# Embedding gate: three of four output-tile pairs by seven half products in place of eight, their operand sums formed in the last down projection, the fourth pair by column halves at both ends

## The chip, the cores and the metric

The kernel runs on one core of a Trainium2 chip. The metric is device microseconds of one execution; the time before is the median of three runs, 1333.55 us (1332.72 to 1333.56). All matmuls run on TensorE (PE in the profile); VectorE is DVE, ScalarE is ACT, GpSimd is POOL, and SP is the engine that issues most DMAs. The kernel is written in a tile framework that tracks tiles, places the semaphores and sets the order of each engine's instructions with a scheduler of its own; the order is fixed when the program is built, and each engine works through its list in that order.

## The reference, cut to what matters

One step of a one-layer decoder for 64 sampled tokens and 512 prompt tokens, 576 rows in all, with a model width of 1024. After the token mixers the layer does this:

```python
hf = rmsnorm(h, w['norm_ffn'])
h = h + (jax.nn.silu(hf @ w['w_gate']) * (hf @ w['w_up'])) @ w['w_down']
gate = jax.nn.sigmoid(rmsnorm(h, w['norm_ple']) @ w['w_ple_gate'])
h = h + gate * (p.astype(h.dtype) @ w['w_ple_proj'])
...
y_prompt = rmsnorm(hp, norm_final)
```

The change is in the line of `gate`, a product of 576 x 1024 by 1024 x 1024 in float32. The product `p @ w_ple_proj` is made much earlier in the kernel and waits in DRAM as eight tiles `pp_d`.

## The kernel before

Everything is held transposed: 128 partitions are 128 features, and the 576 tokens lie along the free axis. A tensor of 1024 features is eight tiles of 128 x 576. The residual is `hs[0..7]`.

**Float32 by three passes.** A float32 operand is split into a high part `hi` (rounded to float32r by an ACT copy) and a low part `lo` (the source less `hi`, by DVE or POOL, or, where the engine is given as "D", by a negated ACT copy and an accumulating DMA that POOL issues). A product is the sum of hi·hi, hi·lo and lo·hi. `split` (L193) and `below` (L185) do this; all ACT copies have line L93, and the `lo` parts lines L191 and L213. For a tile of 128 outputs over 1024 inputs this is 8 input tiles times 3 passes.

**The gate and up projections** of the feed-forward part are made by `seven` (L1443): two output tiles at a time form a 2 x 2 block matrix (two halves of the inputs, `a11` to `a22` being 128 x 512 blocks of the weights), the tokens are cut in two halves `N1` and `N2` of 288, and the eight half products are made as seven, with sums of weight blocks (`s1`, `s2`, `s4`, and `a21` in place) and sums of the data (`T1` to `T4`, split once ahead). Each half product is `product` (L1428), 12 matmuls of 288 columns at line L1432. The seven are made in the order 1, 6, 4, 7, 5, 2, 3. Two PSUM tiles take them: `ab` (parts a, b) and `cd` (parts c, d), each 1024 columns. Step 7 adds into b, which step 6 wrote and DVE then read (`e[2]`, L1477); DVE reads b again as `e[3]` (L1483) after step 7; step 2 adds into a, in the same tile as b, and in the built program its first matmul waits for that read. In the same way the first matmul of step 5 (part c) waits for DVE's read of part d. `weave` (L1502) keeps two such blocks in flight; there are nine gate and nine up blocks, in two stretches, each followed by a down projection, `down` (L1520), of 8 tiles with 72 or 60 matmuls of 288 columns (L241). Its result is scaled on DVE (`dn`), added to `hs[c]` on POOL (L1526), and in the last `down` the function `after` (L1306) makes the split operand `xhi`, `xlo` of the next product and its squares `hsq`, which POOL sums up.

**The embedding gate** (L1541 to L1601) is made directly: for the token columns 0 to 320, and then for 320 to 576, all eight output tiles one after the other, each with 24 matmuls (L1577, L1578, L1579). Weights are loaded and split in the first pass and kept for the second. For each tile DVE scales by the reciprocal norm (L1583), ACT takes the sigmoid, and `embed` multiplies by the tile `pl` of the embedding product (L1556), adds to `hs[c]` (L1557), takes the square and sums it up on POOL (L1563). After each pass the final norm follows: `rstd_by_token` (L329) sums the squares over the partitions by matmuls with one column (L339), takes root and reciprocal, spreads the result over the partitions by transposes (L347), and eight tiles are scaled (six on DVE, L1600, two on POOL, L1598) and stored. For the first pass this lies beside the matmuls of the second.

## Time and profile before

| | us |
|---|---|
| median of three runs | 1333.55 |
| the profiled execution's own time | 1329.48 |
| its span, first to last instruction | 1327.7 |
| last matmul of the down projection begins its last group of four | 1259.17 |
| first matmul of the embedding gate | 1259.69 |
| last matmul of the embedding gate | 1316.30 |
| the weave of the second stretch, one pair of blocks (168 matmuls), from 1148.22 to 1171.20 | 22.98 |

The profiled execution took 1329.48 us, 4.07 less than the median of the runs; 1.78 of it lies outside the span. A timeline row gives the start, the length of the group, the engine, the line, the tiles (output, then inputs), the shape, the count, and in brackets idle time ahead of it with what ended that. Matmuls overlap their neighbours, so that the rate of a series is read from one start to the next and not from the length. The squares' sums (L339) show twice as many records as there are instructions.

### The profile page before, as it was taken

How to read it: one execution, taken by the hardware profiler on the slowest of the kernel's cores; microseconds unless marked ns; L12 is line 12 of the kernel's file. 1: busy time of each engine (PE TensorE's matmuls, PEld its weight loads, DVE VectorE, ACT ScalarE, POOL GpSimd, SP SyncE). 2: the span in 40 equal slices, each digit the busy share in tenths (PEclk: the TensorE clock that was granted, in tenths of full speed). 3: DMA queues.
4: the chain of work that ended last, by engine and by line, in shares of the span. 5: the costliest groups of instructions: out<-in, count | busy, mean ns of one | idle time of the engine just before them, and what ended most of it. 6: DMA issues, size and time to landing. Idle time of an engine off the chain costs nothing.

```text
span 1327.7 us, 26629 instructions
## 1 busy us (share of the span) xinstructions
PE 1224.9 (92%) x10429; PEld 1125.1 (85%) x10429; DVE 885.8 (67%) x1569; ACT 632.0 (48%) x1274; POOL 615.4 (46%) x584
## 2 busy tenths in 40 slices
PE   6897899999989978899989989999999999999997
PEld 5786797889968966788769878999999999999996
DVE  6649665878696876953456576858895138883464
ACT  6565436543654374343444364455553225553363
POOL 5426513642265136122445665647565345654642
PEclk9898999799978979979989989999999999999998
DMA  5322241334232322353454541253342224424322
GB/s 167 127 65 72 78 116 54 98 96 119 73 103 79 83 72 78 103 180 106 132 182 131 201 151 59 78 161 106 98 113 89 81 83 114 116 66 136 99 89 72
DMA packets 96764, 140.29 MB, mean 106 GB/s; under 512 B 34960, under 2 KB 39312, under 8 KB 96640
## 3 DMA queue, kind: packets, MB, share of 16 engines
q1 hardware_dynamic: 93760, 133.36, 32.6%
q0 software_dynamic: 2304, 4.72, 2.1%
q8 instruction: 82, 1.34, 0.4%
q10 hardware_dynamic: 576, 0.52, 0.1%
q14 instruction: 42, 0.34, 0.1%
HBM read 106.10 MB, written 27.75 MB: 101 GB/s over the span
## 4 chain that ended last, share of the span: by engine, by line
PE 58%; DVE 19%; ACT 6%; issue 6%; DMA 4%; POOL 3%; SPq 0%; DVEq 0%; ACTq 0%; POOLq 0%
PE lin L241 12%; PE lin L1432 11%; PE lin L228 6%; PE lin L230 6%; PE lin L229 6%; DVE h L402 2%; DVE wl L191 1%; DVE Tt L683 1%; DVE tmp L681 1%; DVE wlo L213 1%; PE lin L1577 1%; PE lin L1578 1%; PE lin L1579 1%; DVE suv L838 1%; DMA raw<-wts 1%
## 5 line engine op out<-in xcount | busy, mean ns | idle before, releaser
L213 POOL TENSOR_TENSOR wlo<-raw,whi 128x512 fp32r<-128x512 f32 (+1 forms) x92 | 125.8, 1368 | 303.6 <-ACT whi L93 235.0
L228 PE MATMUL lin<-xhi,whi 128*128 128x288 f32 (+1 forms) x784 | 242.1, 309 | 2.8 <-ACT whi L93 2.2
L230 PE MATMUL lin<-xhi,wlo 128*128 128x288 f32 (+1 forms) x784 | 240.2, 307 | 4.0 <-POOL wlo L213 2.3
L229 PE MATMUL lin<-xlo,whi 128*128 128x288 f32 (+1 forms) x784 | 239.6, 306 | 1.2 <-POOL xlo L191 1.1
L93 ACT ACTIVATE whi<-raw 128x512 fp32r<-128x512 f32 (+1 forms) x200 | 123.2, 616 | 211.0 <-PE lin L241 90.0
L228 PEld LDWEIGHTS lin<-xhi,whi 128*128 128x128 f32 (+1 forms) x784 | 149.5, 191 | 10.1 <-ACT whi L93 2.6
L230 PEld LDWEIGHTS lin<-xhi,wlo 128*128 128x128 f32 (+1 forms) x784 | 149.4, 191 | 7.9 <-POOL wlo L213 2.7
L229 PEld LDWEIGHTS lin<-xlo,whi 128*128 128x128 f32 (+1 forms) x784 | 149.4, 191 | 6.5 <-POOL xlo L191 2.4
L213 DVE TENSOR_TENSOR wlo<-raw,whi 128x512 fp32r<-128x512 f32 (+1 forms) x108 | 82.1, 761 | 74.2 <-PE lin L241 36.0
L1432 PE MATMUL lin<-T,wh 128*128 128x288 f32 x576 | 87.3, 296 | 2.0 <-DVE e L1477 1.3
L1432 PEld LDWEIGHTS lin<-T,wh 128*128 128x128 f32 x576 | 80.0, 189 | 3.2 <-DVE e L1477 1.6
L93 ACT ACTIVATE wh<-raw 128x512 fp32r<-128x512 f32 x72 | 45.1, 628 | 52.5 <-PE lin L1432 35.4
L191 POOL TENSOR_TENSOR wl<-raw,wh 128x512 fp32r<-128x512 f32 x36 | 57.3, 1592 | 11.7 <-ACT wh L93 6.2
L191 DVE TENSOR_TENSOR wl<-sw,wh 128x512 fp32r<-128x512 f32 x53 | 49.9, 941 | 9.3 <-ACT wh L93 5.2
L241 PE MATMUL lin<-ah,whi 128*128 128x288 f32 x352 | 54.7, 294 | 0.0
L241 PE MATMUL lin<-al,whi 128*128 128x288 f32 x352 | 54.4, 294 | 0.0
L241 PE MATMUL lin<-ah,wlo 128*128 128x288 f32 x352 | 54.2, 294 | 0.0
L681 DVE TENSOR_TENSOR tmp<-L,Tt 72x30 f32<-72x30 f32 (+14 forms) x120 | 49.9, 416 | 3.2
L1432 PE MATMUL lin<-T,wl 128*128 128x288 f32 x288 | 49.8, 297 | 0.6 <-DVE wl L191 0.6
L241 PEld LDWEIGHTS lin<-ah,whi 128*128 128x128 f32 x352 | 49.3, 188 | 0.0
L241 PEld LDWEIGHTS lin<-al,whi 128*128 128x128 f32 x352 | 49.2, 188 | 0.0
L241 PEld LDWEIGHTS lin<-ah,wlo 128*128 128x128 f32 x352 | 49.2, 188 | 0.0
(437 smaller groups left out, 3265.7 us busy)
## 6 DMA issues: line engine op xcount, KB each, us to landing
raw<-wts SPq DMA_DIRECT2D x271, 256.0 KB, 2.6
S<-s_wkv SPq DMA_DIRECT2D x8, 512.0 KB, 5.1
hd<-s_ssm SPq DMA_DIRECT2D x8, 512.0 KB, 4.6
o_ssm_s<-hd SPq DMA_DIRECT2D x8, 512.0 KB, 2.8
xbc_d<-E SPq DMA_DIRECT2D x12, 288.0 KB, 2.1
x<-xT SPq DMA_DIRECT2D x8, 288.0 KB
gate_d<-g SPq DMA_DIRECT2D x8, 288.0 KB, 2.5
bv_d<-rw SPq DMA_DIRECT2D x8, 288.0 KB
```

Source lines behind the costliest of these rows:

```text
L93: return S.activation(out, in_, func, bias=bias, scale=scale)
L191: eng.tensor_tensor(lo, src, hi.bitcast(F32), ALU.subtract)
L213: eng.tensor_tensor(lo[:, 0:n], raw[:, 0:n], hi[:, 0:n].bitcast(F32), ALU.subtract)
L228: T.matmul(ps[:, a:b], whi, xhi[:, a:b], start=first, stop=False)
L229: T.matmul(ps[:, a:b], whi, xlo[:, a:b], start=False, stop=False)
L230: T.matmul(ps[:, a:b], wlo, xhi[:, a:b], start=False, stop=last)
L241: T.matmul(ps[:, a:e], (hi, lo)[p][:, i * P:(i + 1) * P], xs[k + i][q][:, a:e], start=n == k + i == 0, stop=n == 2 and k + i == nk - 1, sk ...
L402: V.scalar_tensor_tensor(h[:], E[:, i:i + 600], w(i), h[:], ALU.mult, ALU.add)
L681: V.tensor_tensor(o, L[:, jx:jx + 1, jx + 1:32].to_broadcast([NB, jx, n]), Tt[:, 0:jx, jx:jx + 1].to_broadcast([NB, jx, n]), ALU.mult)
L683: V.tensor_tensor(Tt[:, 0:jx, jx + 1:32], Tt[:, 0:jx, jx + 1:32], o, ALU.subtract)
L838: V.scalar_tensor_tensor(dst, sv[h, jj, 0, e], PC[h, jj, 7 + g:8 + g], dw[h, jj], ALU.mult, ALU.add)
L1432: T.matmul(ps, (hi, lo)[p][:, k * P:(k + 1) * P], OPS[n][k][q], start=first and p == q == k == 0, stop=p == 1 and k == 3, skip_group_check ...
```

## The change

The gate's eight output tiles become four pairs. Pairs 0, 1 and 2 (tiles 0 to 5) are made by a new function `joined`, which does what `seven` does for the gate projection, one block after the other, with the same `product`. Tiles 6 and 7 are made by `plain` as before, with 24 matmuls each for `N1` ahead of the joined pairs and 24 each for `N2` at their end. All matmuls of the gate are now 288 columns wide: 3 x 84 joined and 4 x 24 plain, 348, against 192 of 320 and 192 of 256 columns before.

The sums of the data `T1` to `T4` are made by a new function `operands`, for each of the last four tiles of the last down projection. The embedding, the square and its sum are put off (`put_off`, `catch_up`, with a table `CU` of how many to take up after each step); for tiles 0 to 3 the adds to `hs[c]` go from DVE to POOL, and the squares are summed in two pairs only, so that six tiles of squares go into each final norm where three went before. The final norm of `N1` is written between the two plain tiles of `N2`. In the weave, the split weights get four buffers in place of three and the small tiles `e` six in place of eight, since the pool `cm` now lives on to the end; the embedding tiles `pl`, the plain weights and the squares take the places of the feed-forward tiles `ah`, `al`, and so are loaded only when the last down projection has read those. In the last down projection's last tile the add to `hs[7]` goes from POOL to DVE. The early load of the square root's table ahead of the last final norm is left out.

```diff
     def product(ps, w, n, first, eng):
-        hi, lo = split(w[:], cm, ("wh", "wl"), [P, 512], lo_eng=eng, bufs=3)
+        hi, lo = split(w[:], cm, ("wh", "wl"), [P, 512], lo_eng=eng, bufs=4)
...
+    CU = ((0,0,1,1,0,0,0),(0,1,1,0,0,0,0),(0,1,1,0,1,1,1))
+    PLE_ENG = ((V, V, G, V, "D", G, V), (V, V, G, V, "D", G, V), (V, V, G, V, "D", G, V))
...
+    def operands(k):
+        t0, t1, t2, t3, t4 = (cm.tile([P, HALF], F32, tag="e", name=nm("t"), bufs=6) for _ in range(5))
+        ha, hb = hs[k], hs[k + 4]
...
+        act(t0[:], ha[:, N2], AF.Identity, scale=ga)
+        V.scalar_tensor_tensor(t1[:], ha[:, N1], ga, t0[:], ALU.mult, ALU.subtract)
+        V.scalar_tensor_tensor(t2[:], hb[:, N2], gb, t1[:], ALU.mult, ALU.add)
+        V.scalar_tensor_tensor(t3[:], hb[:, N2], gb, t0[:], ALU.mult, ALU.subtract)
+        V.scalar_tensor_tensor(t4[:], hb[:, N1], gb, t2[:], ALU.mult, ALU.subtract)
...
-            G.tensor_tensor(hs[c][:], hs[c][:], t[:], ALU.add)
+            (V if last and c == 7 else G).tensor_tensor(hs[c][:], hs[c][:], t[:], ALU.add)
             if last:
-                after(c, hs[c], "norm_ple", pools[-1], "f", 9, st)
+                after(c, hs[c], "norm_ple", fp, "f", 6, st)
+                if c > 3:
+                    operands(c - 4)
...
+    def embed(c, t, sq, w, eng=V):
+        act(t[:, w], t[:, w], AF.Sigmoid)
+        V.tensor_tensor(t[:, w], t[:, w], PL[c][:, w], ALU.mult)
+        eng.tensor_tensor(hs[c][:, w], hs[c][:, w], t[:, w], ALU.add)
+        if c < 7:
+            act(sq[:, w], hs[c][:, w], AF.Square)
+        else:
+            V.tensor_tensor(sq[:, w], hs[c][:, w], hs[c][:, w], ALU.mult)
...
+            if c in (0,2):
+                G.tensor_tensor(SQ[c][:], SQ[c][:], SQ[c + 1][:], ALU.add)
+                summed.append(c + 1)
...
+        for n, step in enumerate("1647523"):
...
+            elif step == "7":
+                product(b, a21, "T3", False, on["7"])
+                e[3] = kt()
+                V.tensor_tensor(e[3][:], b, e[1][:], ALU.add)
+                joins(sb, 2 * p + 1, N1, d, e[3], SQ[2 * p + 1])
...
+    t6, t7 = spare("al8", "pg"), spare("ah9", "pg")
+    for i, t in enumerate((t6, t7)):
+        plain(i, N1, t)
+    for p in range(3):
+        joined(p)
+    plain(0, N2, t6)
+    catch_up(5)
+    store(N1, False)
+    plain(1, N2, t7)
+    catch_up(5)
+    store(N2, True)
```

The scheduler puts the instructions in a new order at three places that matter below. The first is on PE, in the weave of the second stretch. Here `lin_13224` is the tile `ab` of one block and `lin_13379` that of the next one; `T_1592` and `T_1593` are the high and the low part of `T3`, so that these rows are step 7, and `wh_13381`, `wl_13382` are the split weights of the next block's step 1. First the rows that leave their place:

```order
 L1432 MATMUL lin_13080<-xhi_9757,wl_13282 128x288
 L1432 MATMUL lin_13225<-T_1594_10206,wl_13301 128x288 x4
-L1432 MATMUL lin_13224<-T_1592_10204,wh_13326 128x288 x4
-L1432 MATMUL lin_13224<-T_1593_10205,wh_13326 128x288 x4
-L1432 MATMUL lin_13224<-T_1592_10204,wl_13327 128x288 x4
 L1432 MATMUL lin_13379<-xhi_9471,wh_13381 128x288
 L1432 MATMUL lin_13379<-xhi_9511,wh_13381 128x288
```

And, eight matmuls further on in the same piece of the list of PE, where they now stand:

```order
 L1432 MATMUL lin_13379<-xlo_9553,wh_13381 128x288
 L1432 MATMUL lin_13379<-xlo_9594,wh_13381 128x288
+L1432 MATMUL lin_13224<-T_1592_10204,wh_13326 128x288 x4
+L1432 MATMUL lin_13224<-T_1593_10205,wh_13326 128x288 x4
+L1432 MATMUL lin_13224<-T_1592_10204,wl_13327 128x288 x4
 L1432 MATMUL lin_13379<-xhi_9471,wl_13382 128x288
 L1432 MATMUL lin_13379<-xhi_9511,wl_13382 128x288
```

Step 7 stood ahead of all 12 matmuls of the next block's step 1 and now stands ahead of its last four; right behind those, in both programs, comes step 2 of the block `lin_13224`.

The second place is the end of the list of PE. Before, `lin_15244` is the last tile of the gate, `lin_15281` the final norm of the second pass:

```order
L1579 MATMUL lin_15244<-xhi_14472,wp_14933 128x256
L1577 MATMUL lin_15244<-xhi_14561,wp_14932 128x256
L1578 MATMUL lin_15244<-xlo_14562,wp_14932 128x256
L1579 MATMUL lin_15244<-xhi_14561,wp_14933 128x256
L339 MATMUL lin_15281<-ones,sq_15210 64x1 x4
L339 MATMUL lin_15281<-ones,sq_15243 64x1 x4
L339 MATMUL lin_15281<-ones,sq_15277 64x1 x4
L347 MATMUL lin_15281<-ident,rn_2487_15294 128x128 x2
```

Now `lin_15338` is tile 7 of `N2`, `lin_15275` the final norm of `N1` and `lin_15368` that of `N2`:

```order
L339 MATMUL lin_15275<-ones,sq_14681 64x1 x6
L339 MATMUL lin_15275<-ones,sq_14682 64x1 x6
L339 MATMUL lin_15275<-ones,sq_14683 64x1 x6
L339 MATMUL lin_15275<-ones,sq_14684 64x1 x6
L1604 MATMUL lin_15338<-xhi_14504,wp_14656 128x288
L1602 MATMUL lin_15338<-xhi_14611,wp_14655 128x288
L1603 MATMUL lin_15338<-xlo_14612,wp_14655 128x288
L1604 MATMUL lin_15338<-xhi_14611,wp_14656 128x288
L339 MATMUL lin_15368<-ones,sq_14679 64x1 x2
L339 MATMUL lin_15368<-ones,sq_14681 64x1 x6
L339 MATMUL lin_15368<-ones,sq_14682 64x1 x6
L347 MATMUL lin_15275<-ident,rn_2516_15312 128x128 x3
```

The sums of the first half's final norm now stand four matmuls ahead of the end of the gate, and its transposes behind it. Two more groups of them stand further ahead, 6 and 16 matmuls long, so that 46 matmuls of one column lie ahead of the gate's last product where 18 lay before.

The third place is the end of the list of DVE. Before, `pg_15269` is the gate of the last tile and `h_9161` the residual `hs[7]`:

```order
L1583 TENSOR_TENSOR pg_15269<-lin_15244,rstd_14622 128x256
L1556 TENSOR_TENSOR pg_15269<-pg_15269,pl_14583 128x256
L1557 TENSOR_TENSOR h_9161<-h_9161,pg_15269 128x256
L1561 TENSOR_TENSOR sq_15277<-h_9161 128x256
L344 RECIPROCAL rn_2487_15294<-rn_2487_15294 128x2
L1600 SCALAR_TENSOR_TENSOR h_8706<-h_8706,pv,lin_15281 128x256
```

Now `pg_14686` is the gate of tile 7, and `lin_15275` the spread norm of `N1`:

```order
L1607 TENSOR_TENSOR pg_14686<-lin_15338,rstd_14712 128x288
L1575 TENSOR_TENSOR pg_14686<-pg_14686,pl_14663 128x288
L1576 TENSOR_TENSOR h_9161<-h_9161,pg_14686 128x288
L1679 SCALAR_TENSOR_TENSOR h_8706<-h_8706,pv,lin_15275 128x288
L1679 SCALAR_TENSOR_TENSOR h_8771<-h_8771,pv,lin_15275 128x288
L1679 SCALAR_TENSOR_TENSOR h_8901<-h_8901,pv,lin_15275 128x288
L1679 SCALAR_TENSOR_TENSOR h_9031<-h_9031,pv,lin_15275 128x288
L1679 SCALAR_TENSOR_TENSOR h_9096<-h_9096,pv,lin_15275 128x288
L1679 SCALAR_TENSOR_TENSOR h_9161<-h_9161,pv,lin_15275 128x288
L1580 TENSOR_TENSOR sq_14684<-h_9161 128x288
L344 RECIPROCAL rn_2520_15405<-rn_2520_15405 128x3
```

The six scalings of the first half's final norm have come to stand between the last tile's add to the residual and the square of it.

More of the change, by code (lines that the diff above doesn't have):

```diff
@@ L1597, in hybrid_step, with store @@
+    def store(w, last):
+        ps = rstd_by_token(tuple(q for i, q in enumerate(SQ) if i not in summed), 1.0 / D, w.start, w.stop)
+        rl = ft("rs")
+        act(rl[:, w], ps)
+        for c in range(8):
+            h = hs[c][:, w]
+            if c in (2, 4):
                 act(h, h, AF.Copy, scale=par("norm_final", c))
-                G.tensor_tensor(h, h, rl, ALU.mult)
+                G.tensor_tensor(h, h, rl[:, w], ALU.mult)
             else:
                 V.scalar_tensor_tensor(h, h, par("norm_final", c), ps, ALU.mult, ALU.mult)
-            (nc.scalar if a and c % 2 else nc.sync).dma_start(A["yT"][c, :, a:b], h)
+            (nc.scalar if last and c % 2 else nc.sync).dma_start(A["yT"][c, :, w], h)
```

147 lines of the change are left out of this document (91 added, 56 removed).

## The prediction

> **What bounds the kernel now.** I read the page first, then the busy time by stretches around the change, then PE's timeline at their ends.
>
> ```profile
> span 1327.7 us, 26629 instructions
> ...
> PE 1224.9 (92%) x10429; PEld 1125.1 (85%) x10429; DVE 885.8 (67%) x1569; ACT 632.0 (48%) x1274; POOL 615.4 (46%) x584
> ```
>
> ```profile
> core 0: us, PE busy (x) PEld busy (x) DVE busy (x) ACT busy (x) POOL busy (x), PEclk, DMA share, GB/s
> 1148.22:1171.20 22.98, 22.74 (x169) 22.38 (x169) 20.62 (x32) 12.45 (x23) 14.03 (x11) 1.00 0.47 119
> 1259.69:1316.42 56.73, 56.08 (x470) 54.66 (x468) 33.08 (x63) 29.63 (x58) 21.39 (x20) 1.00 0.26 80
> 1316.42:1327.70 11.28, 1.85 (x28) 1.15 (x26) 4.30 (x11) 2.55 (x5) 1.48 (x3) 0.63 0.29 93
> ```
>
> PE is busy for 92% of the span. The second row is one pair of blocks of the weave, the third the whole gate, the fourth what follows its last product. In the weave and in the gate PE has the full clock (1.00) and is almost never idle; but in the weave DVE is busy for 20.62 of 22.98 us, in the present gate for only 33.08 of 56.73. So the gate is bound by the number of its products, and there is idle time on DVE and POOL that another form can use up. The last 11.28 us are a chain through DVE and ACT, with PE at 1.85.
>
> PE's timeline gives the rates:
>
> ```profile
> 1158.92 0.69 PE L1432 MATMUL lin<-xhi,wl 128*128 128x288 f32 x4
> 1159.57 0.77 PE L1432 MATMUL lin<-xhi,wh 128*128 128x288 f32 x4
> ...
> 1169.74 0.69 PE L1432 MATMUL lin<-xlo,wh 128*128 128x288 f32 x4
> 1170.27 0.69 PE L1432 MATMUL lin<-xhi,wl 128*128 128x288 f32 x4
> 1171.20 0.77 PE L1432 MATMUL lin<-xhi,wh 128*128 128x288 f32 x4 [0.24 <-DVE e L1483]
> ...
> 1277.80 0.31 PE L1578 MATMUL lin<-xlo,wp 128*128 128x320 f32 x1
> 1283.96 0.31 PE L1578 MATMUL lin<-xlo,wp 128*128 128x320 f32 x1
> ...
> 1292.10 0.52 PE L339 MATMUL lin<-ones,sq 128*64 128x1 f32 x12
> 1292.55 0.38 PE L1577 MATMUL lin<-xhi,wp 128*128 128x256 f32 x1
> ...
> 1301.07 0.28 PE L1577 MATMUL lin<-xhi,wp 128*128 128x256 f32 x1
> 1303.22 0.28 PE L1577 MATMUL lin<-xhi,wp 128*128 128x256 f32 x1
> ```
>
> From start to start, 42 products of 320 columns took 6.16 us, 0.1467 each; 18 of 256 took 2.15, 0.1194 each; four of 288 took 0.53 (1169.74 to 1170.27), 0.1325 each. Six column sums (twelve records) took 0.45, 0.075 each.
>
> **The change, part by part.** The sum is made against the profiled execution, 1329.48 us; the median of the runs lies 4.07 higher, and I carry the difference over unchanged. 0.2% is 2.7 us, about what a measurement of this kernel can tell from no change.
>
> Products: before 192 x 0.1467 + 192 x 0.1194 = 51.1; after 348 x 0.1325 = 46.1. That is -5.0, all of it on the path, since PE hardly idles there.
>
> Column sums: 46 stand ahead of the last product in place of 18, because only two pairs of squares are summed beforehand: 28 x 0.075 = +2.1. The three transposes of the first half leave the stretch: -0.3, estimated at a product's rate or less.
>
> Waits inside the stretch. Of the 56.73 us, 51.1 are products and 18 x 0.075 = 1.4 column sums; 4.2 are left, of which the 20 sums of the down projection's squares (1.5) and eight transposes (some 0.6) are work, so about 2.1 are waits and switches. What the joined pairs will wait has no row of its own; the nearest ones are those of the weave, which uses the same products in the same order:
>
> ```profile
> 1167.94 0.67 DVE L191 TENSOR_TENSOR wl<-sw,wh 128x512 fp32r<-128x512 f32 x1
> 1168.54 0.68 DVE L191 TENSOR_TENSOR wl<-raw,wh 128x512 fp32r<-128x512 f32 x1
> 1169.14 1.54 DVE L1498 TENSOR_TENSOR sa<-sa,rstd 128x288 f32<-128x288 f32 x1
> 1170.61 0.45 DVE L1483 TENSOR_TENSOR e<-lin,e 128x288 f32<-128x288 f32 x1
> ```
>
> ```profile
> 1168.69 1.67 POOL L1453 TENSOR_TENSOR sw<-raw,sw 128x512 f32<-128x512 f32 x1 [3.23 <-DVE wl L191]
> ```
>
> ```profile
> 939.97 1.93 PE L1432 MATMUL lin<-T,wh 128*128 128x288 f32 x8 [1.35 <-DVE e L1477]
> ```
>
> The rows 1170.27 and 1171.20 show the weave's wait at step 2: four products last 0.53, the next one starts 0.93 later, so 0.40 is lost until DVE has read `e[3]`; at the other block's step 2 it is 0.12 (1158.92 to 1159.57, 0.65), 0.52 in a pair of blocks. The weave has a second block to work on while it waits. A joined pair has none: step 7 waits for the read of `e[2]`, 2 for that of `e[3]`, 5 and 3 for those of d and c, and only the following pair's first eight products stand in between at one place. The lower bound for 252 such products is the weave's rate, 0.52 x 252 / 168 = 0.8. The upper one comes from the weave's start, where one wait alone was 1.35 (row 939.97): at two such waits in each pair, 8. I take 4.3, between the two and nearer the first: DVE is in order, and behind each put-off embedding it stands at the sigmoid's result from ACT, with `e[3]` queued behind it; ACT has a tile's square ahead of the copies that split the next pair's `a11`. Against the 2.1 of before this is +2.2, with ends -1.3 and +5.9.
>
> The front seam I cost at nothing. The sums for `T2` to `T4` of the last down tile come behind `hs[7]`, whose add moves from POOL to DVE:
>
> ```profile
> 1259.88 0.76 DVE L1525 TENSOR_TENSOR dn<-lin,rstd 128x576 f32<-128x576 f32 x1 [0.61 <-PE lin L241]
> ```
>
> ```profile
> 1260.72 1.44 POOL L1526 TENSOR_TENSOR h<-h,dn 128x576 f32<-128x576 f32 x1 [2.66 <-DVE dn L1525]
> ```
>
> On DVE the add, three sums and the low parts, all of 576 columns or fewer and so none above the 0.76 of the first row, are done some 5 us after 1260.6; the first product that needs them stands behind 48 plain products (6.4), the sums and step 1 (1.6), about 1268. The embedding tiles and plain weights, whose places come free only when the last down projection has read them, have the same cover. If it is gone, the price is what those loads take over, up to 3.
>
> The tail. At the end DVE's list now has six scalings of the first half between the add to `hs[7]` and its square:
>
> ```profile
> 1316.69 0.43 DVE pg L1583
> 1317.14 0.42 ACT pg L93
> ...
> 1318.51 0.43 DVE sq L1561
> 1318.99 0.42 PE lin L339 x8
> ```
>
> ```profile
> 1301.44 2.84 DVE L1600 SCALAR_TENSOR_TENSOR h<-h,pv,lin 128x320 f32<-128x320 f32 x6 [1.87 <-ACT rs L93]
> ...
> 1321.16 2.44 DVE L1600 SCALAR_TENSOR_TENSOR h<-h,pv,lin 128x256 f32<-128x256 f32 x6 [1.26 <-ACT rs L93]
> ```
>
> ```profile
> 1293.91 1.28 ACT L93 ACT_TABLE_LOAD   x1
> ```
>
> Six took 2.84 at 320 and 2.44 at 256 columns, so 2.64 at 288. They lie on the path: the square, the last column sums and the whole second norm wait for them. On ACT, the root of the first norm and a table load (1.28) stand ahead of the last sigmoid, which began 0.72 after the last product before (1317.14 less 1316.42): root 0.2 before the last product at the earliest, 0.3 long, and 1.28 is about 1.35 after it, so up to +0.6; I take +0.4. The wider columns add some 0.15. Tail +3.2. The table load that is no longer called early (1.28) comes behind the first norm's spread and is hidden by the 2.64. The lower bound is +0.5, if the column sums of tile 7 were to find something else late; the upper +4, if sixteen stores of a half tile queue up at the end.
>
> The weave. Step 7 now ends eight products later, and four (0.53) in place of twelve (1.59) lie between its end and step 2. Step 2 keeps its place, and so its wait depends on when DVE reads `e[3]`. That read began at 1170.61, and step 7 would now end at about 1170.4: not later than DVE is ready. A fourth buffer lets splits run ahead. With nine pairs of blocks in the two stretches, 0.52 each, all that there is to gain is -4.7; if each of eighteen reads comes 0.2 later, the loss is 3.6. I take a fifth of the gain, -1.0, since DVE's 20.62 of 22.98 is unchanged.
>
> The sum: -5.0 + 2.1 - 0.3 + 2.2 + 3.2 - 1.0 = +1.2, so 1333.55 + 1.2 = 1334.7 us.
>
> **The rivals.** (a) Faster: the weave loses half its waits (-2.4), and the joined pairs run at the weave's rate (-1.3). For it: `operands` does its work in the last down projection, so the joined pairs need no more data sums than the weave. Against it: one block in flight. -5.0 + 2.1 - 0.3 - 1.3 + 3.2 - 2.4 = -3.7: 1329.8.
>
> (b) Slower: DVE and POOL bound the joined stage. The scaling of 288 columns at 1169.14 took 1.54, while in the row ahead of it 512 columns took 0.60 from start to start; it lies within POOL's operation of 1168.69 and ends with it. So operations of the two engines that read SBUF twice go one after the other. From the order, the joined stretch holds on POOL eight such operations of 512 columns (1.29 by the group below) and six of 576 (1.44): 19.0; on DVE eleven of 512 at 0.60, eight of 576 and five of 288 (0.68 and 0.34 by length): 13.7. Together 32.7 in 252 x 0.1325 = 33.4 us of products, 98%; in the weave it is 8 x 1.29 + 14 x 0.60 + 0.68 + 4 x 0.34 = 20.7 in 22.98, 90%.
>
> ```profile
> L1452 POOL TENSOR_TENSOR raw<-raw,raw 128x512 f32<-128x512 f32 x2 | 2.6, 1288 | 2.6 <-DVE sw L1450 2.6
> ```
>
> It decides from the point where a split or an `e` waits behind POOL in each pair; then the waits reach the upper bound, 8: 1.2 + 3.7 = +4.9, 1338.4. For it: the 98%, and embedding adds that come just when the next pair's splits are due. Against it: DVE's reads of PSUM don't share that time, and splits may run four buffers ahead. [...]
>
> That the change doesn't do what it says is excluded: the order holds 252 and 96 products of the gate in place of 384.
>
> **How the numbers follow.** The forecast 0.45, (a) 0.27, (b) 0.28. The forecast's own range, with its waits, tail and weave off by one microsecond each, is 1332 to 1337. The range that reaches into both rivals is 1328.5 to 1340.0: (a) with half of what the weave has left beyond it, (b) with a tail at its upper end. Faster by over 0.2% means under 1330.9, which is (a); slower means over 1336.2, which is (b).
>
> **What would show it.** In the profile after: 348 products at 0.1325 from the end of the last down projection; PE idle between joined steps of about 4.3 in all, with `e`, `sa` or `sb` named; from the last product to the end 14.5 in place of 11.28, with six scalings ahead of the last square; the weave's pair at 22.87 in place of 22.98. A stretch of the gate shorter than 53 or a pair of the weave under 22.7 would make it (a); a stretch over 59 with DVE operations of more than 1.4 us before PE's waits, (b).

## The result, and the profile after

The changed kernel took 1349.85 us (median; 1346.63 to 1355.45), the kernel before beside it 1333.13 (1327.97 to 1333.56). The ratio is 1.0139, with a 95% interval of 1.0094 to 1.0184: slower by some 17 us, where 1334.7 was forecast and 1340.0 was the upper end.

The head of the page and the same stretches as before: one pair of blocks of the weave, the gate, the tail.

```profile
span 1350.1 us, 26799 instructions
...
PE 1231.8 (91%) x10478; PEld 1130.6 (84%) x10478; DVE 932.8 (69%) x1609; ACT 647.6 (48%) x1300; POOL 637.2 (47%) x594
```

```profile
core 0: us, PE busy (x) PEld busy (x) DVE busy (x) ACT busy (x) POOL busy (x), PEclk, DMA share, GB/s
1144.79:1167.96 23.17, 22.66 (x168) 22.41 (x169) 21.87 (x32) 12.66 (x23) 14.73 (x10) 1.00 0.44 116
1270.84:1334.31 63.47, 56.90 (x487) 54.43 (x485) 49.70 (x75) 34.60 (x65) 26.98 (x21) 0.95 0.20 57
1334.31:1350.06 15.75, 3.71 (x60) 2.86 (x58) 7.73 (x18) 4.31 (x8) 3.30 (x4) 0.56 0.45 150
```

The gate takes 63.47 us for fewer products, not 56.73. PE was busy for 56.08 of it before and is busy for 56.90 now, and it idles for 6.6 us in place of 0.65; DVE is busy for 49.70, no longer for 33.08. The granted clock in the gate is 0.95, where it was 1.00. The tail is 15.75, not 11.28. This pair of the weave has not become shorter: 23.17, where 22.98 was the row before; what the weave as a whole did comes with the account below.

The two profiled executions (1329.48 and 1351.96) differ by 22.5 us, more than the medians. To see how much of that is the change I cut both traces at five places: the first product of the first weave (895.67 before, 903.85 after), the first product of the second weave (1081.67, 1090.63), the first product of the gate (1259.69, 1270.84), its last (1316.30, 1334.18), the end of the span (1327.67, 1350.06). The differences of the stretches are +8.2 ahead of the first weave, +0.8 in the first weave and the down projection behind it, +2.2 in the second weave and the last down projection, +6.7 in the gate, +4.5 in the tail. The 8.2 lie where both programs do the same work; over all traces of this study that stretch took between 895.7 and 907.8, and it says nothing on the change. The last four sum to +14.2.

Where PE idles in the gate, its timeline shows (the bracket is the idle time, with what ended it):

```profile
1274.81 0.40 PE L1604 MATMUL lin<-xhi,wp 128*128 128x288 f32 x1 [1.96 <-DVE wp L213]
...
1291.16 0.83 PE L1432 MATMUL lin<-xhi,wh 128*128 128x288 f32 x4 [2.06 <-ACT wh L93]
...
1292.74 1.16 PE L1432 MATMUL lin<-xhi,wh 128*128 128x288 f32 x4
1293.70 1.16 PE L1432 MATMUL lin<-xlo,wh 128*128 128x288 f32 x4
...
1306.31 0.80 PE L1432 MATMUL lin<-xhi,wh 128*128 128x288 f32 x4 [0.63 <-DVE e L1649]
...
1321.81 0.77 PE L1432 MATMUL lin<-xhi,wh 128*128 128x288 f32 x4 [1.49 <-DVE e L1649]
```

Three long waits stand out: at the front among the first plain tile's products, at the start of the second pair, and at step 2 of the third pair. And there is a second loss behind them: from 1292.74 to 1293.70 four products take 0.96, 0.24 each, in place of 0.13. The windows on both sides of that wait give the clock beside it:

```profile
1288.00:1291.10 3.10, 1.10 (x9) 0.87 (x7) 3.10 (x6) 1.62 (x4) 1.49 (x1) 1.00 0.28 85
1291.90:1295.10 3.20, 3.20 (x15) 3.20 (x14) 2.48 (x4) 0.77 (x2) 1.28 (x1) 0.50 0.32 82
```

PE idles for two thirds of the first window at a clock of 1.00; in the second it is busy throughout at 0.50. The clock record has two such stretches of 3.41 us in the gate (from 1291.8 and from 1322.5), each right behind a long wait, and each costs a little under half its length: 14 products that take 0.24 and not 0.133 lose 1.5 us. Counted at the half, the gate without them is 63.35 - 3.41 = 59.9 us; by the products it is 60.3.

The front. DVE is late with the low part of the plain weights (L213, `wp`), which it begins at 1274.07, since the sums of the data stand ahead of it in its list and POOL's work at the same time stretches them. One such sum, and POOL beside it:

```profile
1270.38 1.69 DVE L1531 SCALAR_TENSOR_TENSOR t<-h,pv,t 128x288 f32<-128x288 f32 x1
```

```profile
1270.11 1.65 POOL L1317 TENSOR_TENSOR hsq<-hsq,hsq 128x576 f32<-128x576 f32 x1
```

The sum `t` took 0.51 one tile later (1278.75), here 1.69; it ends behind POOL's `hsq` (1270.11 and 1.65), which it stands beside. The second pair's start is ACT's list:

```profile
1287.37 0.78 ACT L93 ACTIVATE pg<-pg 128x288 f32<-128x288 f32 x2
1288.05 0.62 ACT L93 ACTIVATE wh<-sw 128x512 fp32r<-128x512 f32 x1
1290.15 0.44 ACT L93 ACTIVATE sq<-h 128x288 f32<-128x288 f32 x1 [1.48 <-DVE h L1576]
1290.50 0.61 ACT L93 ACTIVATE wh<-raw 128x512 fp32r<-128x512 f32 x1
```

The copy `wh` of 1290.50, for which PE waits, has its source ready; it stands behind the square, which waits for DVE's add to the residual. At the third pair it is DVE:

```profile
1317.77 2.02 DVE L1664 TENSOR_TENSOR sa<-sa,rstd 128x288 f32<-128x288 f32 x1
1320.54 0.76 DVE L1575 TENSOR_TENSOR sa<-sa,pl 128x576 f32<-128x576 f32 x1 [0.75 <-ACT sa L93]
1321.22 0.45 DVE L1649 TENSOR_TENSOR e<-lin,e 128x288 f32<-128x288 f32 x1
```

```profile
1317.85 1.61 POOL L191 TENSOR_TENSOR wl<-raw,wh 128x512 fp32r<-128x512 f32 x1
```

The scaling of 288 columns takes 2.02 (POOL's `wl` runs through it), then DVE stands for 0.75 at the sigmoid, multiplies, and only then makes the read `e[3]` that step 2 waits for. The tail, on DVE and ACT:

```profile
1336.44 0.46 DVE L1575 TENSOR_TENSOR pg<-pg,pl 128x288 f32<-128x288 f32 x1 [1.23 <-ACT pg L93]
1336.93 1.02 DVE L1576 TENSOR_TENSOR h<-h,pg 128x288 f32<-128x288 f32 x1
1337.88 2.63 DVE L1679 SCALAR_TENSOR_TENSOR h<-h,pv,lin 128x288 f32<-128x288 f32 x6
1340.43 0.44 DVE L1580 TENSOR_TENSOR sq<-h 128x288 f32<-128x288 f32 x1
```

```profile
1333.10 1.28 ACT L93 ACT_TABLE_LOAD   x1
1334.39 0.26 ACT L93 ACTIVATE rn<-lin,eps_t 128x3 f32<-128x3 f32 x1
1334.67 1.28 ACT L93 ACT_TABLE_LOAD   x1
1335.96 0.44 ACT L93 ACTIVATE pg<-pg 128x288 f32<-128x288 f32 x1
```

The last sigmoid begins 1.65 us behind the last product (1335.96 less 1334.31), where it was 0.72; the add takes 1.02 in place of 0.43, beside a scaling on POOL; then come the six scalings, 2.63; the square begins 6.12 behind the last product, where it was 2.09.

### The profile page after: what moved, and what is told of

Read it like the earlier page. It is cut to its first block, busy times and chain, and to the rows that moved or that the text cites. A ratio compares the mean times of both kernels' runs of the same rounds, so it can differ in the third digit from the quotient of the medians.

```text
span 1350.1 us, 26799 instructions
## 1 busy us (share of the span) xinstructions
PE 1231.8 (91%) x10478; PEld 1130.6 (84%) x10478; DVE 932.8 (69%) x1609; ACT 647.6 (48%) x1300; POOL 637.2 (47%) x594
## 4 chain that ended last, share of the span: by engine, by line
PE 55%; DVE 20%; ACT 7%; issue 6%; DMA 4%; POOL 3%; DVEq 0%; SPq 0%; ACTq 0%; POOLq 0%
PE lin L1432 12%; PE lin L241 11%; PE lin L228 6%; PE lin L230 6%; PE lin L229 6%; DVE h L402 2%; DVE Tt L683 1%; DVE wl L191 1%; DVE tmp L681 1%; DVE wlo L213 1%; DMA raw<-wts 1%; DVE suv L838 1%; ACT L93 1%; DVE xlo L1310 1%; PE lin L620 1%
## 5 line engine op out<-in xcount | busy, mean ns | idle before, releaser
L213 POOL TENSOR_TENSOR wlo<-raw,whi 128x512 fp32r<-128x512 f32 (+1 forms) x94 | 128.7, 1369 | 304.0 <-ACT whi L93 239.1
L213 DVE TENSOR_TENSOR wlo<-raw,whi 128x512 fp32r<-128x512 f32 (+1 forms) x106 | 79.5, 751 | 67.8 <-ACT whi L93 34.2
L1432 PE MATMUL lin<-T,wh 128*128 128x288 f32 x672 | 104.0, 299 | 3.9 <-ACT e L93 3.8
L1432 PEld LDWEIGHTS lin<-T,wh 128*128 128x128 f32 x672 | 94.7, 191 | 5.0 <-ACT e L93 4.8
L191 POOL TENSOR_TENSOR wl<-raw,wh 128x512 fp32r<-128x512 f32 x42 | 66.4, 1580 | 13.7 <-ACT wh L93 9.7
L93 ACT ACTIVATE wh<-raw 128x512 fp32r<-128x512 f32 x84 | 52.2, 627 | 37.9 <-PE lin L1432 34.1
L93 ACT ACTIVATE wh<-sw 128x512 fp32r<-128x512 f32 x63 | 39.5, 627 | 42.9 <-PE lin L1432 35.1
L1432 PE MATMUL lin<-T,wl 128*128 128x288 f32 x336 | 58.8, 298 | 0.2 <-POOL wl L191 0.2
L191 DVE TENSOR_TENSOR wl<-sw,wh 128x512 fp32r<-128x512 f32 x59 | 53.2, 901 | 8.3 <-ACT wh L93 7.9
L1432 PE MATMUL lin<-xhi,wh 128*128 128x288 f32 x252 | 45.8, 305 | 6.8 <-ACT wh L93 2.3
L1432 PEld LDWEIGHTS lin<-T,wl 128*128 128x128 f32 x336 | 50.0, 191 | 0.4 <-POOL wl L191 0.4
```

The source lines that it names most:

```text
L93: return S.activation(out, in_, func, bias=bias, scale=scale)
L191: eng.tensor_tensor(lo, src, hi.bitcast(F32), ALU.subtract)
L213: eng.tensor_tensor(lo[:, 0:n], raw[:, 0:n], hi[:, 0:n].bitcast(F32), ALU.subtract)
L1432: T.matmul(ps, (hi, lo)[p][:, k * P:(k + 1) * P], OPS[n][k][q], start=first and p == q == k == 0, stop=p == 1 and k == 3, skip_group_check ...
```

## The experiments

Whole times of these kernels scatter by several us, so the stretches of the traces carry the readings, and the whole times are given beside them. All rows are read as the cuts above: "II" from the first product of the second weave to the first of the gate, "gate" to its last product, "half" the time in the gate at half clock, "net" the gate less half of that (some 0.2 too low for each stretch of 3.4, as just said), "tail" from the last product's start to the end of the span.

| kernel | II | gate | half | net | tail | median us | ratio to before (95%) |
|---|---|---|---|---|---|---|---|
| before | 178.02 | 56.61 | 0 | 56.6 | 11.37 | | |
| changed | 180.21 | 63.35 | 6.8 | 59.9 | 15.87 | 1349.85 | 1.0139 (1.0094 to 1.0184) |
| e1_weave | 179.04 | 56.62 | 0 | 56.6 | 11.07 | 1335.98 | 1.0016 (0.9993 to 1.0040) |
| e2_no_operands | 178.95 | 60.70 | 6.8 | 57.3 | 15.90 | 1344.25 | 1.0080 (1.0048 to 1.0113) |
| e3_square_act | 180.57 | 63.36 | 6.8 | 60.0 | 14.22 | 1347.78 | 1.0104 (1.0057 to 1.0151) |
| e4_late | 180.23 | 64.21 | 10.2 | 59.1 | 15.88 | 1348.63 | 1.0107 (1.0073 to 1.0141) |
| e5_pool_short | 180.00 | 58.30 | 6.8 | 54.9 | 15.71 | 1343.28 | 1.0083 (1.0057 to 1.0110) |
| e6_store_first | 179.99 | 60.33 | 3.4 | 58.6 | 15.59 | 1343.96 | 1.0082 (1.0054 to 1.0109) |
| e7_wp_pool | 179.98 | 64.88 | 10.2 | 59.8 | 15.89 | 1350.97 | 1.0134 (1.0098 to 1.0169) |
| e8_all | 180.00 | 61.79 | 6.8 | 58.4 | 15.96 | 1347.06 | 1.0105 (1.0054 to 1.0157) |
| e9_adds_dve | 179.96 | 60.44 | 3.4 | 58.7 | 16.44 | 1345.76 | 1.0113 (1.0082 to 1.0144) |
| e10_no_scalings | 179.82 | 63.95 | 6.8 | 60.5 | 13.21 | 1352.28 | 1.0147 (1.0129 to 1.0164) |
| e11_mended | 179.71 | 61.07 | 6.8 | 57.7 | 14.88 | 1341.37 | 1.0063 (1.0039 to 1.0087) |

The theory from these rows: PE waits at three places for engines that work their lists in order, each long wait is followed by a half clock, and the tail pays for the scalings and tables. The rival, which the prediction had priced as (b): DVE and POOL hold each other up, as at the sum `t` above (1.69 beside POOL's `hsq`, 0.51 one tile later), and that bounds the joined pairs.

**e1_weave**, the weave's part alone, on the kernel before:

```diff
-        hi, lo = split(w[:], cm, ("wh", "wl"), [P, 512], lo_eng=eng, bufs=3)
+        hi, lo = split(w[:], cm, ("wh", "wl"), [P, 512], lo_eng=eng, bufs=4)
-        kt = lambda: cm.tile([P, HALF], F32, tag="e", name=nm("e"), bufs=8)
+        kt = lambda: cm.tile([P, HALF], F32, tag="e", name=nm("e"), bufs=6)
```

> The kernel before with one part of the change alone: four buffers in place of three for the split weights and six in place of eight for the small tiles of the half products; the gate is the direct one of before. Both theories put the changed kernel's extra time into the gate and what lies around it, so both expect here a time within 3 us of the kernel before, and 178.0 us plus or minus 1 from the first product of the second weave to the first product of the gate, where before took 178.02 and the changed kernel 180.21. If this stretch comes out at 180 or more, the buffers and not the sums of the data are what the last down projection pays for.

The whole time is that of the kernel before within the interval, and gate and tail are untouched. Stretch II is 1.02 longer, just outside the 178.0 plus or minus 1. This isn't the weave: the first 900 of the stretch's 1320 products take 123.04 here and took 123.17 before, and the last 420, in the last down projection, take 56.00 and took 54.84 (more on this in the last section). So the buffers bring nothing that can be measured in the whole time, neither the gain of 1.0 that was forecast nor a loss that explains the result.

**e2_no_operands**, the sums of the data left out:

```diff
-                if c > 3:
-                    operands(c - 4)
```

> The changed kernel without the sums of the data T1 to T4 in the last down projection (left out; the joined pairs read what the gate projection left in those tiles, so the output is not the reference's). Theory: DVE is behind at the seam because those 36 operations stand in its list, and the plain weights' low part waits behind them. Then the 2.26 us step at the fifteenth product of the gate goes, the two 0.36 us steps in the last down projection go, and the stretch from the second weave's first product to the gate's first falls from 180.21 to about 178.5, the gate from 63.35 to about 60.5; in all about 4 us less than the changed kernel. Rival: the plain weights come late from memory, or their split stands behind the add to the residual that moved to DVE; then the 2.26 us step stays above 1.5.

Stretch II falls by 1.26, the gate by 2.65, as the theory had it, and the wait among the first plain products is gone: no idle time of PE over 0.8 us is left in the gate ahead of the second pair. The sums cost 3.9 us at the seam, where they had been costed at nothing.

**e3_square_act**, tile 7's square on ACT:

```diff
-        if c < 7:
-            act(sq[:, w], hs[c][:, w], AF.Square)
-        else:
-            V.tensor_tensor(sq[:, w], hs[c][:, w], hs[c][:, w], ALU.mult)
+        act(sq[:, w], hs[c][:, w], AF.Square)
```

> The changed kernel with the squares of tile 7 made on ACT, as those of tiles 0 to 6, and not on DVE. Theory: in the tail the square stands behind six scalings on DVE (2.63 us) and everything after it waits; with the square on ACT the second norm's reciprocal is due when the scalings end, at about 6.2 us after the last product in place of 7.8, and the tail from the last product to the end falls from 15.9 to about 14.4, the gate unchanged. Rival: the tail is long because of the two table loads on ACT ahead of the last sigmoid and one more behind it; then the square on ACT delays the last table load by as much as it gains and the tail stays at 15.5 or more.

The tail falls to 14.22, near the 14.4 of the theory, and the gate stays. ACT and DVE of this kernel's tail:

```profile
1341.85 0.44 ACT L93 ACTIVATE sq<-h 128x288 f32<-128x288 f32 x1 [1.28 <-DVE h L1576]
1342.31 1.28 ACT L93 ACT_TABLE_LOAD   x1
1343.60 0.26 ACT L93 ACTIVATE rn<-lin,eps_t 128x3 f32<-128x3 f32 x1
```

```profile
1341.74 2.63 DVE L1676 SCALAR_TENSOR_TENSOR h<-h,pv,lin 128x288 f32<-128x288 f32 x6
1344.29 0.16 DVE L344 RECIPROCAL rn<-rn 128x3 f32<-128x3 f32 x1
```

The scalings now lie beside the square and a table load; the reciprocal still waits for the last of them, so 1.65 of the 2.63 comes back.

**e4_late**, the plain tiles' embedding later:

```diff
-    CU = ((0,0,1,1,0,0,0),(0,1,1,0,0,0,0),(0,1,1,0,1,1,1))
+    CU = ((0,0,0,0,1,1,0),(0,1,1,0,0,0,0),(0,1,1,0,1,1,1))
```

> The changed kernel with the embedding of the two plain tiles of the first half taken up two steps later in the first joined pair (the table's first row 0,0,0,0,1,1,0 in place of 0,0,1,1,0,0,0). On ACT the square of tile 6 then stands behind the copy that splits the first block of the second pair, not ahead of it; PE's list is the same. Theory: PE's 2.06 us of idle time at the second pair's start comes from ACT working in order, and the half clock that follows for 3.4 us (1.7 lost) comes from that idle time. Then the wait falls under 0.7, the thirteen products behind it run at 0.13 in place of 0.24, and the gate falls from 63.35 to about 60.0. Rival, DVE and POOL bound the joined stage by their shared time: the wait moves to a later step and the gate falls by less than 1.

PE's rows of the second pair's start, and of the front:

```profile
1287.91 0.80 PE L1432 MATMUL lin<-xhi,wh 128*128 128x288 f32 x4 [0.19 <-ACT wh L93]
...
1290.13 0.79 PE L1432 MATMUL lin<-xhi,wh 128*128 128x288 f32 x4 [0.89 <-DVE e L1649]
```

```profile
1270.73 0.49 PE L1604 MATMUL lin<-xhi,wp 128*128 128x288 f32 x1 [1.97 <-DVE wp L213]
1271.01 0.45 PE L1602 MATMUL lin<-xhi,wp 128*128 128x288 f32 x1
1271.25 0.45 PE L1603 MATMUL lin<-xlo,wp 128*128 128x288 f32 x1
```

The wait of 2.06 is down to 0.19 and the half clock behind it is gone: the square's place in ACT's list was its cause. But the net gate falls by only 0.8 (a wait of 0.89 at the first pair's step 2, which had none, takes its place in part, and the third pair's grows from 1.49 to 1.78), and the gate as a whole rises, because now the front's wait of 1.97, which was as long in the changed kernel (1.96) and not followed by anything, is followed by 6.8 us at half clock. Both theories are half right here: the wait's cause is shown, the gain of 3.4 isn't, and which wait drew a half clock was not the same in the two executions.

**e5_pool_short**, POOL's work out of the joined pairs:

```diff
-        G.tensor_tensor(a21[:], a11[:], a21[:], ALU.subtract)
-        G.tensor_tensor(s4[:], a12[:], s2[:], ALU.subtract)
+        G.tensor_tensor(a21[:, 0:8], a11[:, 0:8], a21[:, 0:8], ALU.subtract)
...
+        if eng is G and short:
+            hi = cm.tile([P, 512], F32R, tag="wh", name=nm("wh"), bufs=4)
+            act(hi[:], w[:])
+            lo = hi
```

> The changed kernel with POOL's work taken out of the joined pairs: the adds to tiles 0 to 3, the two sums of squares and the difference of weight blocks on POOL cover 8 columns each, the sum s4 and the low parts that POOL makes are left out (the products use s2 and the high part in their place), so the output is not the reference's; PE does as many products. Rival, the shared time of DVE and POOL bounds the joined stage: then every DVE operation there takes 0.4 to 0.8 us, the waits of 0.8 and 1.56 us at the second products of the second and third pair go with the half clock behind the latter, and the gate falls from 63.35 to 59 or less. Theory, the places in the lists of ACT and DVE: the wait of 2.2 us at the second pair's start stays above 1.2, since ACT's square stands ahead of the copy there, and the 2.26 us at the front stays; the gate stays above 60.5.

The groups of DVE's costliest line in the joined stretch, first of the changed kernel, then of this one (count, busy time, mean ns of one):

```profile
L191 DVE TENSOR_TENSOR wl<-sw,wh 128x512 fp32r<-128x512 f32 x5 | 6.9, 1382 | 0.1
```

```profile
L191 DVE TENSOR_TENSOR wl<-sw,wh 128x512 fp32r<-128x512 f32 x5 | 3.4, 686 | 0.1
```

Without POOL beside it the same five operations take 0.69 each and not 1.38, and the net gate falls by 5.0 to 54.9. Not all of that is waiting. The gate of this kernel, to be read against the row of the changed one above:

```profile
1272.13:1330.56 58.43, 55.22 (x443) 52.92 (x441) 38.08 (x73) 32.45 (x61) 7.63 (x13) 0.94 0.19 57
```

PE idles for 3.2 us in place of 6.6, so 3.4 of the 5.0 is idle time. Some 1.4 is work that has only moved: the scheduler put 22 column sums (44 of 487 records) behind the last product. The waits of 0.63 and 1.49 at step 2 are gone, the one at the second pair's start is 0.98 (the step is 1.28, above the 1.2 of the theory, though only just), and the front's is unchanged. The theory's bound of 60.5 for the gate failed and the rival's 59 held; with the sums put back the gate would be 59.7, between the two. So shared time is likely the larger part of what the joined pairs lose, 3.4 of the 4.4 us that PE idled there. This run doesn't divide it from results of POOL that are no longer waited for, nor, at the third pair, from the order: PE's list is that of the changed kernel up to there, and then has the plain products in other places.

**e6_store_first**, the first half's norm ahead of the plain tiles:

```diff
+    store(N1, False)
     plain(0, N2, t6)
     catch_up(5)
-    store(N1, False)
     plain(1, N2, t7)
```

> The changed kernel with the final norm of the first half written ahead of the first plain tile of the second half, not between the two. The scheduler now puts tile 7's square ahead of the first norm's six scalings on DVE, and one table load on ACT at the end in place of three. Theory: both orders cost the tail, the scalings 2.63 us and the tables nearly 1 us ahead of the last sigmoid; the tail falls from 15.9 to about 13.3 (the direct kernel's 11.4, and the first norm's scalings in DVE's list ahead of the second's, partly beside the column sums). Rival: the sixteen stores at the end set the tail; then it stays above 14.5.

The tail is 15.59, not 13.3. DVE and PE there:

```profile
1328.12 2.64 DVE L1679 SCALAR_TENSOR_TENSOR h<-h,pv,lin 128x288 f32<-128x288 f32 x6 [1.08 <-ACT rs L93]
1330.68 0.17 DVE L344 RECIPROCAL rn<-rn 128x3 f32<-128x3 f32 x1
```

```profile
1323.29 2.84 PE L339 MATMUL lin<-ones,sq 128*64 128x1 f32 x90
```

The square now comes ahead of the scalings (at 1325.35), but the scheduler has put 45 column sums (90 records, 2.84 us) behind the last product, so that the first norm's scalings begin late, and the second norm's reciprocal, whose root was done at 1329.60, waits for them until 1330.68. The rival's mechanism, the stores, isn't what is seen; the expectation failed because the sums moved onto the path. The gate is shorter here (net 58.6), since sums left it.

**e7_wp_pool** and **e8_all**. The first makes all low parts of the plain weights on POOL, the second adds that to the late embedding, a later place for the third pair's second embedding, and the first half's norm ahead:

```diff
+    only[0] = G
     WP = [wload(4, *(spare(f"a{p}{f}", "wp", (P, 512), F32R) for p in "hl")) for f in (10, 11, 0, 1)]
...
-    CU = ((0,0,1,1,0,0,0),(0,1,1,0,0,0,0),(0,1,1,0,1,1,1))
+    CU = ((0,0,0,0,1,1,0),(0,1,1,0,0,0,0),(0,1,0,1,1,1,1))
```

> The changed kernel with all low parts of the plain weights made on POOL; DVE has two operations of 0.68 us fewer at the seam. Theory: the 2.26 us step among the first plain products is the place of that low part in DVE's list, behind the sums of the data; it falls under 0.5 and the gate by about 2 us, if half clocks are counted apart. Rival: DVE itself is late for xlo and the sums, and the time comes back at the next place where PE needs them (the residual's last tile, then the reciprocal norm): the gate falls by less than 0.7.

> The changed kernel with four of its orders mended together: the two plain tiles' embedding later as in the run before with the late square, the third pair's embedding of tile 2 one step later (behind the read that step 2 waits for), the plain weights' low parts on POOL, the first half's norm ahead of the plain tiles. If the waits named so far are all that the change lost, the gate takes 63.35 - 2.2 - 1.9 - 1.2 - 3.4 (the two half clocks) = 54.7, or 56.4 with one half clock left, and the tail 13.3; with the weave and the last down projection as in the changed kernel, 2.5 us slower than the kernel before in the same clock. Rival: waits move on to the next place, and the gate stays above 58.

In both the rival is right. In e7_wp_pool PE's wait at the front comes back in pieces, the two longest of them:

```profile
1272.90 0.61 PE L1603 MATMUL lin<-xhi,wp 128*128 128x288 f32 x1 [1.27 <-ACT wp L93]
...
1274.26 0.61 PE L1605 MATMUL lin<-xhi,wp 128*128 128x288 f32 x1 [0.50 <-POOL wp L213]
```

```profile
1271.89 0.44 ACT L93 ACTIVATE T<-t 128x288 fp32r<-128x288 f32 x1 [2.72 <-DVE t L1528]
1272.24 1.14 ACT L93 ACTIVATE wp<-raw 128x512 fp32r<-128x512 f32 x2
```

ACT's copies of the plain weights stand behind the split of a sum that DVE has not made yet: it is DVE that is late, whatever engine makes the low parts. The net gate is 59.8, as in the changed kernel. e8_all has the same at its front; the third pair's wait at step 2 is gone, but there is a new one of 1.82 for POOL's sum of squares in the last stretch (brought by the earlier norm); the gate is 61.8, net 58.4, not 54.7 to 56.4, the rival's "above 58", and the tail is 15.96, not 13.3.

**e9_adds_dve**, the adds to tiles 0 to 3 on DVE again:

```diff
-                    put_off(2 * p + 1, sb, SQ[2 * p + 1], slice(0, NT), G)
+                    put_off(2 * p + 1, sb, SQ[2 * p + 1], slice(0, NT), V)
-                    put_off(2 * p, sa, SQ[2 * p], slice(0, NT), G)
+                    put_off(2 * p, sa, SQ[2 * p], slice(0, NT), V)
```

> The changed kernel with one part undone: the adds to the residual's tiles 0 to 3 stay on DVE, as in the kernel before, in place of POOL; all else is as in the change, and the result too. The run without POOL's work showed that the shared time of DVE and POOL costs the joined pairs most of their waits; this one tells whether it is the adds that do so. If the adds on POOL (four of 1.44 us, against 0.68 on DVE) are what stretches DVE, the waits of 0.8 and 1.56 us at the second products of pairs 2 and 3 fall by half and the gate, with half clocks counted apart, falls from 59.9 to 58.5 or less. If it is the low parts and sums of weight blocks that POOL makes, the adds on DVE only lengthen DVE's list ahead of the reads that PE waits for, and the gate stays at 59.9 or grows by up to 1.5.

Both waits at step 2 are gone from PE's timeline. The five low parts of DVE's group shown above take 0.86 each here, where they took 1.38:

```profile
L191 DVE TENSOR_TENSOR wl<-sw,wh 128x512 fp32r<-128x512 f32 x5 | 4.3, 860 | 0.0
```

The net gate is 58.7 (1.2 less), just short of the 58.5 set for it; the tail grew by 0.6. Up to the third pair PE's list is that of the changed kernel, so the second pair's wait of 0.63 went with the adds; around the third pair the scheduler moved plain products and column sums, and that its 1.49 came from the adds is not shown. So the adds are a part of the shared time, and putting them on POOL cost the gate more than it saved in the tail, but they are not all of what e5_pool_short removed.

**e10_no_scalings**, the first half's eight scalings left out. Other than its expectation says, this kernel kept the adds on POOL, as in the change:

```diff
-            if c in (2, 4):
+            if not last:
+                pass
+            elif c in (2, 4):
```

> The changed kernel with the adds on DVE as in the run beside it, and without the eight scalings of the first half's final norm (left out: the first half is stored unscaled); its column sums, root, table loads, transposes and stores stay. The tail from the last product to the end was 15.87. Theory: the scalings' 2.63 us lie wholly on the path, and what is left over the direct kernel's 11.4 is the table load ahead of the last sigmoid: the tail falls to 13.2, with the last sigmoid 1.6 us behind the last product. Rival: the stores of both halves set the end: the tail stays above 14.5.

The tail is 13.21: the 2.66 less are the scalings' 2.63. So it isn't the stores that set the end. (The whole time is not shorter, 1352.28; in this trace the stretch ahead of the first weave, where the programs do the same work, is the longest of all, 907.8.) Of the 4.5 by which the change lengthens the tail, 2.6 are scalings; the late sigmoid is 0.9 (1.65 against 0.72) and the stretched add 0.6 (1.02 against 0.43).

**e11_mended**, three of these edits together, the adds on DVE, the late embedding (with the third pair's second one a step later) and tile 7's square on ACT:

> The changed kernel with the three orders mended that single runs have shown to matter: the adds to tiles 0 to 3 on DVE, the plain tiles' embedding two steps later (and the third pair's second one step later), tile 7's square on ACT. From the parts: second weave and last down projection 180.0 as before; gate 60.4 less 1.7 for the half clock and 1.6 for the wait at the second pair, 57.1, if the front's 2 us of idle time is not followed by a half clock, up to 60.5 if it is; tail 16.4 less 1.6, 14.8. From the first weave's first product to the end 437.5 to 441, where the changed kernel had 446.2 and the kernel before 432.0, so still 5 to 9 us slower than before. If the parts do not add up (a rival: each mended wait only uncovers the next), it stays above 443.

From the first weave's first product (901.68) to the end (1342.78) it takes 441.1, against 446.2 and 432.0. The net gate is 57.7 (57.1 was worked out), the tail 14.88 (14.8). The front's wait of 1.98 was followed by 6.8 us at half clock, the case that the expectation gave with 60.5; the gate is 61.07. So the parts add up within 0.6, and the mended kernel is 1.0063 times the kernel before (1.0039 to 1.0087): better than the change, and still slower than what it replaces.

## Why the prediction was wrong, point by point

**Products, right.** -5.0 was forecast. The 348 products are there; at full clock the joined ones run at 0.133 each (eight in 1.07, from 1285.74 to 1286.81), and e5_pool_short, with most waits of the joined pairs taken away, has a net gate 1.7 below that of before (1.3 by the products), with 3.2 us of idle time in it against 0.65.

**Column sums, right in kind.** 28 more were priced at 2.1. They run at 0.064 in long groups (45 in 2.84 us), which makes 1.8.

**Waits of the joined pairs, right in size, and the rival was a part of their mechanism.** 4.3 was taken; PE's idle times there are 2.06 + 0.25 + 0.63 + 1.49 = 4.4. The 2.06 is the place that the prediction named (ACT's square ahead of the split of the next pair's `a11`), shown by e4_late. For the rest rival (b) named DVE and POOL taking turns. At the second pair (0.63) that is borne out by e5_pool_short and, for the adds, by e9_adds_dve. At the third pair (1.49) it is argued: the wait went in both, but with another order of PE's list, and in e6_store_first and e8_all waits of 1.60 and 1.82 for POOL's sum of squares stand there in its place. The sum of 32.7 us of work in 33.4 of products should have been read as a bound that is reached, not as one that is just missed, since the work isn't spread evenly. That the two engines take turns the trace of before shows in the weave: of nine `sa<-sa,rstd` (L1498, which reads no PSUM) the eight that lie beside a tensor operation of POOL took 1.18 to 1.55 and ended 0.31 to 0.33 behind POOL's, the ninth took 0.45; all eighteen `e<-lin,e` (L1483, `lin` in PSUM) took 0.44 to 0.46, seventeen of them beside such an operation. The 1382 against 686 ns for the same five `wl` agree with that.

**The front seam, wrong.** The step that failed is "The front seam I cost at nothing". It counted DVE's work for the last tile at the durations of quiet rows, some 5 us and "none above the 0.76", though the kernel before has one of 1.98 just ahead of its gate:

```profile
1256.69 1.98 DVE L1310 SCALAR_TENSOR_TENSOR xlo<-h,pv,xhi 128x576 fp32r<-128x576 f32 x1
```

It left out that three more tiles' sums and low parts had been queued up ahead of that work and that POOL's adds and sums of squares run at the same time. And it gave the plain weights the 48 plain products as their cover, while it is these products that need the weights' low parts, and one of those low parts stands in DVE's list behind the sums. The sums of the data cost 2.65 in the gate and 1.26 ahead of it (e2_no_operands), 3.9 where nothing stood. The price of up to 3 for the cover being gone was in neither the sum nor the range; it was meant for late loads, so that it lies near the 2.65 is luck.

**Half clock, missing.** No step had it. It costs 3.0 us by the products (3.4 at the half) in the gate of the changed kernel's trace, and, at the half, between 1.7 and 5.1 in every other kernel with joined pairs. The sign stood in a row that the prediction quoted for another purpose: at 939.97 eight products, behind 1.35 us of idle time, have a length of 1.93, where eight at full clock have 1.23; the clock record of that trace has a half-clock stretch of 3.41 us from 940.43. A wait on PE was priced at its own length, and its price was that and, behind 17 of the 25 waits counted at the end, a stretch of 3.4 or 6.8 us at half clock, which costs some 1.5 or 3 us more.

**The tail, undersized.** +3.2 was forecast, +4.5 came. The six scalings were priced at 2.64 and e10_no_scalings measures 2.66. The table loads were taken at 0.4 and cost 0.9, above the 0.6 that was their bound: ACT's root waited for a table load that stood behind a square and a scaling of another tile (the load at 1333.10), so that it ended 0.3 us behind the last product and not ahead of it. The add stretched by POOL, 0.6, was not seen.

**The weave, a gain that hardly came.** -1.0 was forecast. In stretch II the first 900 products take 122.98 in the changed kernel and 123.04 in e1_weave, 123.17 before, though the pair shown above is 0.2 longer. The first weave with its down projection takes 186.78 and 186.46, 186.00 before, with 3.41 us at half clock in each. That is +0.6 and +0.3 in all, in single traces, and too little to fix a sign.

Summed over these: 1.2 forecast, and above it 2.65 and 1.26 for the front, 3.0 for the half clock, 1.3 for the tail, and 1.9 for what else stretch II took (0.8 of gain that did not come there, 1.1 of a slower rate in the last down projection, for which see the end): 11.3 of the 14.2 that the stretches show. Of the rest 0.8 lies in the first weave and its down projection, and the other 2.1 in switches and small waits that were not taken apart. Rival (b) named what the runs do show (1382 against 686 ns), but not the right place for most of the loss.

## What to carry to other kernels

Saving products helps only if PE keeps being fed: before fewer products are bought with more work on two engines that hold each other up (here 1382 ns beside POOL's work, 686 without), add up that shared work over the stretch with the idle time it is to fill, and take a sum near the products' own time as a loss, as the 98% here were. Price a wait of 1.3 us or more on PE with the clock that may follow it: here 17 of 25 waits of 1.26 to 2.06 us were followed by 3.4 or 6.8 us at half clock. When work is moved ahead into a stage that seems to hide it, follow each engine's list through the last tiles, with stretched durations, to the first instruction that the next stage needs.

## What the runs showed of the hardware that was not expected

The half clock follows short idle times, and not each time. In the gates of the eleven traces with joined pairs (the changed kernel, and e2 to e11), PE idled 25 times for between 1.26 and 2.06 us; 17 of these were followed within 2 us by a stretch at half clock of 3.4 or 6.8 us, 8 were not. Of eight front waits of 1.96 to 1.98 us at the same place, four were followed. So the length of the wait alone didn't decide here; where it fell went far to. In each trace the half-clock stretches begin on one grid with a step of 3.413 us (all 16 of the kernel before, all 19 of the changed one; in the latter's gate 1291.79 and 1322.51, nine steps apart). Of the 25 waits, 19 lie within one step, but for 0.1 us at most, and 17 of these were followed by half clock; 6 are cut by the edge of a step into pieces of 0.27 us or more, and none of these was. Over all thirteen traces, a step at full clock in which PE was busy for less than 40% was followed by half clock in 93 of 93 cases (6 of 6 in the trace of before, 8 of 8 in that of the changed kernel), one with 85% or more in 18 of 3880 (1 of 306 and 2 of 299). No wait in these gates was longer than 2.1 us, so that each was shorter than a step. What sets the grid is not shown.

The same clock goes with most of the scatter of this program: ahead of the first weave the time at half clock runs from 112.6 to 153.6 us over the thirteen traces, and a straight line in it accounts for 69% of the variance of that stretch's length. There, where all kernels do the same work, e6_store_first and e10_no_scalings differ by 11.7 us:

```profile
0.00:896.17 896.17, 804.92 (x7271) 712.54 (x7272) 613.96 (x1155) 441.35 (x936) 393.38 (x418) 0.94 0.36 110
```

```profile
0.00:907.83 907.83, 817.72 (x7271) 722.56 (x7272) 613.64 (x1155) 441.52 (x935) 391.58 (x418) 0.92 0.36 109
```

The counts of instructions are equal within one, DVE, ACT and POOL are as busy, and PE is busy for 12.8 us longer at 0.92 in place of 0.94. A difference of a few us between two single executions can't be put down to an edit; the cut stretches can, to about 1 us.

In the kernel before, the last down projection's products run at 0.1300 each from about 1215 on; in e1_weave and e2_no_operands it is 0.1333 throughout, and in the other ten traces up to the waits among the last 80 (read over 40 products at a time). Over some 340 products that is 1.1 us, as much as e1_weave's longer stretch II and half of the +2.2 of the changed kernel's, so it may be the one trace of before and not the change. Its cause stays open; nothing was tried on it.
